# Attention's fixed order in a hybrid decoder layer: turning two steps ahead, scores five units ahead, gate sums apart, queries scaled later

## The chip, the cores and the metric

The kernel runs on one core of one Trainium2 chip. The metric is the device time of one launch in microseconds (us), the median of several runs. The core has a matrix engine (TensorE, PE in the rows; its weight loads are PEld), VectorE (DVE), ScalarE (ACT), GpSimd (POOL) and SyncE (SP), whose queue here issues the DMAs. TensorE writes its results into eight PSUM banks, from which VectorE and ScalarE copy them out.

## The reference

One decoder layer on 1024 tokens of width 1024, in float32:

```
xn   = RMSNorm(x)
proj = xn @ w_in      # attention q, k, v and gates | conv | memory q | 3 merge gates
A = attention over compressed blocks, selected blocks and a window of 512
B = causal depthwise convolution (31 taps), LayerNorm, swish, projection
C = cross-attention into 256 memory tokens
merged = sum over A, B, C of sigmoid(merge gate) * (branch @ its output weight)
h   = x + merged @ w_out
out = h + (silu(RMSNorm(h) @ w_gate) * (RMSNorm(h) @ w_up)) @ w_down
```

Attention has 8 query heads in 2 groups of width 64. With 1024 tokens all 16 selected blocks are taken, so the selected branch is causal attention over all keys. Each branch has its own softmax and its own gate.

## The kernel before, in words

Matrices are split into a high and a low float32r part, and each product is the sum of three products of parts (`mm3`, with `mm` in L153, the line that nearly every matmul has). A transpose is a matmul with the identity (`turn_in`, L733).

The stages are: projections and convolution taps, memory keys and values, memory attention, attention, merge of the three branches, output projection, and the feed-forward part (the last third of the span). The change is in the attention.

The attention works on 8 blocks of 128 tokens (i) times 2 head groups (g). Each (i, g) is a block of five **units**: branch 0 (compressed keys, all four heads at once), branch 1 (selected) in two head pairs, branch 2 (window) in two head pairs. A unit goes through these stations:

- **scores** (`scores`, L758): TensorE multiplies query tiles (`qt`) by keys, in chunks of up to 512 columns, into three PSUM banks (`at=0`). For branch 0 these are the compressed scores (`kcmp`, `qt`). VectorE adds the mask and takes the row minimum of the negated scores out of the bank (L810 and L780: the drains), ScalarE takes the exponential with a row sum (L815, L782), VectorE the reciprocal (L694), and GpSimd scales the tile (L699). The tiles lie in big buffers named `wsl` (three) and `slab`.
- **turning** (`turn_p`, L826): TensorE transposes the tile, two key blocks a **step**, into three other banks (`at=1`). ScalarE casts the high part (L132), VectorE subtracts to get the low part (L133), into a buffer `t`.
- **take** (`take`, L845): TensorE multiplies values by the turned step into the one output bank (`at=2`). The first take of a block is that of branch 0 (`vcmp`). After the last one of a block ScalarE copies half of the bank (L861), VectorE adds the rest (L864), and a DMA stores it to `od`.

Queries: `load_q` (L735) fetches the raw queries of a token block by DMA (L737) and scales them by their norms on VectorE (L738). `doubled` (L740) multiplies by the gain on GpSimd (L742), and `turn_q` (L746) transposes to `qt`. This happens within the window units of the block before.

**Fills.** The merge gates' projections (`gate_steps`, L705, 24 weight units of 128 columns, two halves each) have no hurry. The first 12 units are given to the scheduler with low priority (early gates). The other 12 (late gates) are 192 fill steps of three matmuls each. Eight steps, 24 matmuls, sum into the one bank `pf`; then ScalarE copies it out (L714, `fz`), and the next sum can begin. Their weights `fsl` are split by ScalarE and GpSimd (L133).

**The order.** Inside the attention TensorE's order is written out by hand (`in_row`, L146: each instruction is tied behind the one before). A plan lists entries. In an entry stand part of the scores of unit k, then the turning of the step after the one to be taken, then some fill steps, then one take step of unit k - LAG, with LAG = 4. Before unit 4 entries have no take. How many fill steps an entry gets follows from a level: each entry's own TensorE time is estimated, and fills raise the short ones to the same height (`share`). The other engines' orders are the scheduler's. Work of the next stage, the memory product (`wsl` by `slab`, L1011), is put between by the scheduler where the row's end comes near; its inputs go through the staging buffers `st`, which it shares with the query tiles.

Of the kernel before, what the change touches and what calls it, by code (L numbers as in the profile page):

```python
# [20 lines left out]
NT = S // P  # L21
KT = D // P
# [8 lines left out]
FILL, TAP = 2000000, 1000000  # L31
ORDER = mybir.DependencyInfo(mybir.DependencyClass.NoSync, mybir.DependencyReason.DATA)
N_EARLY = 12
LAG = 4
T_COL, T_MM, T_TURN = 1 / 2400, 0.0133, 0.112
TAP_LEAD = 12
N_MAIN, N_W, N_F = 16, 3, 2

# [2 lines left out]
def hybrid_layer_kernel(  # L41
# [48 lines left out]
    def t2(shape, dt=F32, p=P):  # L90
        return t2p.tile([p] + shape, dt, tag="t2", name=nm("t2"))

    def small(n):
        if n > 8:
            return smp.tile([P, n], F32, tag="smw", name=nm("smw"), bufs=3)
        return smp.tile([P, n], F32, tag="sm", name=nm("sm"))
# [3 lines left out]
    def bank(shape, dt=F32, p=P, at=None):  # L100
        if at is None:
            turn[1] += 1
            at = order[turn[1] % len(order)]
        return psp[at].tile([p] + shape, dt, tag=f"ps{at}", name=nm("ps"))
# [26 lines left out]
    def split(hi, lo, src, eng=None):  # L131
        m = nc.scalar.copy(hi, src)  # L132
        return m, (eng or nc.vector).tensor_tensor(lo, src, hi.bitcast(F32), op=OP.subtract)  # L133
# [18 lines left out]
    def mm(o, a, b, start, stop):  # L152
        m = nc.tensor.matmul(o, a, b, start=start, stop=stop)  # L153
        in_row(m)
        n = 1
        for d in o.shape[1:]:
            n *= d
        products.append((m.ins, n if a.dtype == F32R else 4 * n))
        return m
# [162 lines left out]
    def wide_proj(ws, t):  # L322

        o = bank([512])
        half, a = t // 4, (t % 4) * P
        if t == 0 and len(products) == 0:
            for k0 in (0, 4):
                for hx, hw in ((0, 0), (1, 0), (0, 1)):
                    for k in range(k0, k0 + 4):
                        mm(o, xn(hx, k, half, a, a + P), ws[k // 2][hw][:, k % 2, :], k + hx + hw == 0,  # L330
                           k == KT - 1 and hw == 1)
            return o
        for k in range(KT):
            hi, lo = ws[k // 2]
            mm3(o, xn(0, k, half, a, a + P), xn(1, k, half, a, a + P), hi[:, k % 2, :], lo[:, k % 2, :], k == 0, k == KT - 1)
        return o
# [50 lines left out]
    for u in range(2):  # L387
        w_ = slab([2, 2, 512])
        m, _ = split(w_[:, 0], w_[:, 1], raw_w[u])
# [268 lines left out]
    for t in range(NT):  # L658
        v = wide_proj(ws, t).rearrange("p (s a g d) -> p s a g d", s=2, a=2, g=2)
# [28 lines left out]
    def balanced(n):  # L688
        return [n] if n <= 4 else [n - n // 2, n // 2]
# [45 lines left out]
    def load_q(i):  # L735
        QN[i] = t2([8, 64])
        nc.sync.dma_start(QN[i].rearrange("p h d -> p (h d)"), qraw[1, i])  # L737
        nc.vector.tensor_tensor(QN[i], QN[i], rqn[:, i, :, None].to_broadcast([P, 8, 64]), op=OP.mult)  # L738

    def doubled(i, g):  # L740
        qd = t2([4, 2, 64])
        nc.gpsimd.tensor_tensor(qd, QN[i][:, 4 * g:4 * g + 4, None, :].to_broadcast([P, 4, 2, 64]),  # L742
                                gn[:, 0, None, None, :].to_broadcast([P, 4, 2, 64]), op=OP.mult)
        return qd

    def turn_q(i, g, qd):  # L746
        b = bank([4, P], at=1)
        for h in range(4):
            turn_in(b[:, h, :], qd[:, h].rearrange("p a d -> p (a d)"))
        QT = stage.tile([P, 2, 4, P], F32R, tag="st", name=nm("qt"))  # L750
        split(QT[:, 0], QT[:, 1], b)
        QS[(i, g)] = QT
# [5 lines left out]
    def scores(u, after):  # L758

        i, g, br, hp = u  # L760
        if br == 2:
            nxt = (i, 1) if g == 0 else (i + 1, 0)
            if hp == 0 and nxt[0] < NT:
                if g == 1 and nxt[0] + 1 < NT:
                    load_q(nxt[0] + 1)
                QD[nxt] = doubled(*nxt)
            if hp == 1 and nxt[0] < NT:
                turn_q(*nxt, QD.pop(nxt))
                yield
        QT = QS[(i, g)]  # L770
        if br == 0:
            mn_, den = small(4), small(4)
            b = bank([4, 64], at=0)
            for h in range(4):
                mm(b[:, h, :], QT[:, 0, h, :], kcmp[:, g * 64:(g + 1) * 64], True, False)
                mm(b[:, h, :], QT[:, 1, h, :], kcmp[:, g * 64:(g + 1) * 64], False, True)
            pc = t2([4, 64])
            tiles = [pc[:, h, :] for h in range(4)]
            for h in range(4):
                nc.vector.tensor_tensor_reduce(tiles[h], b[:, h, :], cmask[:, i, :], op0=OP.add, op1=OP.min,  # L780
                                               scale=-0.125, scalar=BIG, accum_out=mn_[:, h:h + 1])
                nc.scalar.activation(tiles[h], tiles[h], AF.Exp, scale=-1.0, bias=mn_[:, h:h + 1],  # L782
                                     accum_out=den[:, h:h + 1])
            softmax_tail(i, g, br, 0, den, tiles)
            after.append((u, tiles))
            yield
            return
        K = KSW[br - 1]
        k0 = 0 if br == 1 else max(0, i - 4)
        nb = i + 1 - k0  # L790
        turn[0] += 1
        pt = (wslab if turn[0] % 5 < 3 else slab)([2, S], F32)
        tiles = [pt[:, h, :nb * P] for h in range(2)]
        mn_, den = small(4), small(2)
        ch = balanced(nb)
        for h in range(2):
            kb, last = k0, None
            for ci, n in enumerate(ch):
                b = bank([512], at=0)[:, :n * P]
                mm(b, QT[:, 0, 2 * hp + h, :], K[:, g, kb * P:(kb + n) * P], True, False)  # L800
                mm(b, QT[:, 1, 2 * hp + h, :], K[:, g, kb * P:(kb + n) * P], False, True)
                if ci == len(ch) - 1:
                    m = strip[:, 768 - n * P:]
                elif br == 2:
                    m = strip[:, :n * P]
                else:
                    m = strip[:, P:(n + 1) * P]
                acc = mn_[:, 2 * h + ci:2 * h + ci + 1]
                o = (kb - k0) * P
                nc.vector.tensor_tensor_reduce(tiles[h][:, o:o + n * P], b, m, op0=OP.add, op1=OP.min,  # L810
                                               scale=-0.125, scalar=BIG if last is None else last, accum_out=acc)
                last = acc
                kb += n
                if ci == len(ch) - 1:
                    nc.scalar.activation(tiles[h], tiles[h], AF.Exp, scale=-1.0, bias=last, accum_out=den[:, h:h + 1])  # L815
                    if h == 1:
                        softmax_tail(i, g, br, 2 * hp, den, tiles)
                        after.append((u, tiles))
                yield

    def turns_of(u):

        nb = nblocks(u)
        return [0] if u[2] == 0 else [min(2, nb - j) for j in range(0, nb, 2)]
# [57 lines left out]
    plan, steps = [], [(u, s) for u in units for s in range(len(turns_of(u)))]  # L882

    def step_time(u, s):
        n = turns_of(u)[s]
        return 4 * T_TURN + 4 * P * T_COL + T_MM if n == 0 else 2 * n * T_TURN + 2 * n * (2 * P * T_COL + T_MM)

    for k in range(len(units) + LAG):
        at = atoms_of(units[k]) if k < len(units) else []
        mine = list(range(len(turns_of(units[k - LAG])))) if k >= LAG else []  # L890
        m = max(1, len(mine)) if mine else len(at)
        for j in range(m):
            part = at[j * len(at) // m:(j + 1) * len(at) // m]
            v = (units[k - LAG], mine[j]) if mine else None
            plan.append((k, len(part), v, sum(part) + (step_time(*v) if v else 0.0)))

    late = (3 * KT - N_EARLY) * 2 * KT
    room = 3 * late * (4 * P * T_COL + T_MM)
# [8 lines left out]
    for _, _, _, c in plan:  # L907
        run += max(0.0, hi_ - c)
        share.append(min(late, int(late * run / room + 0.5)))

    load_q(0)
    load_q(1)
    QD[(0, 0)] = doubled(0, 0)
    row[0] = keys_done
    turn_q(0, 0, QD.pop((0, 0)))
    fills, filled = late_gates(), 0
# [8 lines left out]
    at_step = 0  # L925
    for (k, n_at, v, _), upto in zip(plan, share):
        for _ in range(n_at):
            next(streams[k])
        if v is not None:
            for n in ((0, 1) if at_step == 0 else (at_step + 1,)):  # L930
                if n < len(steps):
                    turn_step(n)
        for _ in range(filled, upto):
            next(fills)
        filled = upto
        if v is not None:
            take(*v, turned.pop(at_step))
            at_step += 1
# [459 lines left out]
```

## Time and profile before

| | |
|---|---|
| median of 3 runs | 1743.81 us (1742.79 to 1748.59) |
| profiled execution | 1743.21 us, span 1741.5 us |
| granted TensorE clock | 1.00 |
| bytes moved by DMA | 211.83 MB |
| attention's row | about 490 to 885 us of the span |

The profile's page gives each engine's busy time. The views of windows, waits, timeline and chain answer for a stretch: busy time by engine, who ended whose idle time, the instructions in order, and the chain of work that ended last. In a row, `out<-in` are the tiles by name, `x6` is the number of merged instructions, and a bracket gives the idle time before the first of them and what ended it. The busy time of a run of matmuls includes the tail of its last one.

### The profile page before, as it was taken

The page shows a single profiled execution, that of the slowest core. Times are in us where ns is not written, and L with a number is a line of the kernel's source. Part 1 is how long each engine was busy: PE and PEld are TensorE (multiplying, and loading weights), DVE is VectorE, ACT ScalarE, POOL GpSimd, SP SyncE. Part 2 cuts the span into 40 slices and gives each one's busy share as a digit, 9 for nine tenths or more (in the row PEclk, how much of TensorE's full clock was granted, in tenths as well). Part 3 has the DMA queues.
Part 4 walks back from the last instruction along what each step waited for, and adds up shares of the span by engine and source line. Part 5 has one row for each costly group of instructions (what it writes and reads, how often), then busy time and mean ns, then how long its engine had stood idle before and what let it go on. Part 6 is the DMA issues. An engine that isn't in the chain of part 4 may idle for free.

```text
span 1741.5 us, 23348 instructions
## 1 busy us (share of the span) xinstructions
PE 1694.7 (97%) x8520; PEld 1420.8 (82%) x8520; DVE 1077.9 (62%) x1839; ACT 736.5 (42%) x1376; POOL 515.1 (30%) x478
## 2 busy tenths in 40 slices
PE   7999999999988999999999999999999999999999
PEld 6887898888767888888888878878888888888887
DVE  6288887687227676766666535765545555457655
ACT  7311534342237766666555424532322322234332
POOL 0000002120136444434103510366556677410000
PEclk9999999999999999999999999999999999999999
DMA  8012433321221111011565413233332445794773
GB/s 275 33 39 85 164 117 119 104 92 47 67 76 41 43 38 55 28 37 50 169 209 169 156 57 107 97 109 109 97 127 91 158 147 174 250 394 149 230 232 123
DMA packets 176729, 211.83 MB, mean 122 GB/s; under 512 B 11284, under 2 KB 113988, under 8 KB 175590
## 3 DMA queue, kind: packets, MB, share of 16 engines
q1 hardware_dynamic: 176614, 210.34, 36.5%
q8 instruction: 67, 1.10, 0.3%
q14 instruction: 48, 0.39, 0.1%
HBM read 155.77 MB, written 54.53 MB: 121 GB/s over the span
## 4 chain that ended last, share of the span: by engine, by line
PE 56%; DVE 5%; ACT 4%; issue 3%; DMA 3%; POOL 1%; ACTq 0%; DVEq 0%; SPq 0%; POOLq 0%
PE ps L153 31%; PE ps L1332 11%; PE pf L153 10%; PE ps L733 3%; PE pf L1332 1%; DMA t<-zd 1%; POOL slab L1020 1%; ACT slab L132 1%; DVE wsl L810 1%; DVE slab L133 1%; DVE t L864 1%; DMA st<-in_w_nsa_out_dram 1%; ACT slab L815 0%; ACT t L132 0%; DMA st<-md 0%
## 5 line engine op out<-in xcount | busy, mean ns | idle before, releaser
L153 PE MATMUL ps<-slab,wsl 128*128 128x512 f32 (+1 forms) x1652 | 368.3, 381 | 1.6 <-DMA wsl<-in_cmp_w_dram 0.9
L153 PEld LDWEIGHTS ps<-slab,wsl 128*128 128x128 f32 x1652 | 300.0, 188 | 63.0 <-issue 1.7
L153 PE MATMUL pf<-slab,fsl 128*128 128x512 f32 x1236 | 334.9, 404 | 13.7 <-ACT fz L714 13.7
L153 PEld LDWEIGHTS pf<-slab,fsl 128*128 128x128 f32 x1236 | 218.3, 189 | 56.0 <-ACT fz L714 20.1
L1228 DVE TENSOR_TENSOR t<-ps,t 128x512 f32<-128x512 f32 x130 | 88.7, 687 | 108.0 <-PE ps L153 104.6
L428 DVE SCALAR_TENSOR_TENSOR slab<-slab,cw 128x1023 f32<-128x1023 f32 (+14 forms) x120 | 152.1, 1267 | 2.1
L133 DVE TENSOR_TENSOR t<-ps,t 128x512 fp32r<-128x512 f32 (+2 forms) x192 | 120.2, 632 | 52.5 <-ACT t L132 49.8
L153 PE MATMUL ps<-slab,fsl 128*128 128x512 f32 x636 | 149.0, 391 | 1.6 <-DVE slab L133 1.6
L132 ACT CAST t<-ps 128x512 fp32r<-128x512 f32 (+2 forms) x192 | 101.9, 537 | 106.4 <-PE ps L733 86.6
L153 PE MATMUL ps<-wsl,slab 128*128 128x512 f32 (+1 forms) x648 | 140.3, 361 | 1.8 <-ACT slab L132 1.7
L153 PEld LDWEIGHTS ps<-slab,fsl 128*128 128x128 f32 x636 | 119.2, 188 | 27.6 <-DVE slab L133 2.0
L153 PEld LDWEIGHTS ps<-wsl,slab 128*128 128x128 f32 x648 | 108.0, 189 | 19.4 <-ACT slab L132 2.1
L153 PE MATMUL ps<-t,slab 128*128 128x256 f32 (+1 forms) x672 | 120.0, 294 | 1.7 <-DVE t L133 1.1
L153 PEld LDWEIGHTS ps<-t,slab 128*128 128x128 f32 x672 | 104.7, 188 | 19.8 <-DVE t L133 5.5
L1332 PE MATMUL ps<-wsl 128*128 128x512 f32 x495 | 118.7, 389 | 0.0
L153 PE MATMUL ps<-slab,slab 128*128 128x512 f32 x480 | 115.8, 392 | 1.7 <-ACT slab L231 1.3
L600 POOL TENSOR_SCALAR t<-t,sm 128x256 f32<-128x256 f32 x32 | 25.5, 815 | 291.2 <-DVE sm L596 261.6
L1332 PEld LDWEIGHTS ps<-wsl 128*128 128x128 f32 x495 | 92.9, 188 | 19.3
L153 PEld LDWEIGHTS ps<-slab,slab 128*128 128x128 f32 x480 | 89.3, 188 | 21.5 <-ACT slab L231 2.2
L133 DVE TENSOR_TENSOR wsl<-st,wsl 128x1024 fp32r<-128x1024 f32 x58 | 74.5, 1284 | 32.3 <-ACT wsl L132 32.1
L153 PE MATMUL ps<-slab,qt 128*128 128x384 f32 (+3 forms) x384 | 87.6, 333 | 6.5 <-DVE sm L810 6.2
L132 ACT CAST wsl<-st 128x1024 fp32r<-128x1024 f32 x59 | 61.8, 1050 | 72.1 <-PE ps L153 41.5
(245 smaller groups left out, 2719.8 us busy)
## 6 DMA issues: line engine op xcount, KB each, us to landing
t<-in_w_down_dram SPq DMA_DIRECT2D x70, 256.0 KB, 3.6
fst<-in_w_in_dram SPq DMA_DIRECT2D x24, 512.0 KB, 3.7
zd<-fz SPq DMA_DIRECT2D x48, 256.0 KB, 2.0
t<-zd SPq DMA_DIRECT2D x24, 512.0 KB, 3.9
st<-in_w_gate_dram SPq DMA_DIRECT2D x22, 512.0 KB, 3.7
st<-in_w_up_dram SPq DMA_DIRECT2D x22, 512.0 KB, 4.2
ad<-t SPq DMA_DIRECT2D x44, 256.0 KB, 2.6
st<-in_w_in_dram SPq DMA_DIRECT2D x20, 512.0 KB, 3.8
```

The source lines that it names most:

```text
L132: m = nc.scalar.copy(hi, src)
L133: return m, (eng or nc.vector).tensor_tensor(lo, src, hi.bitcast(F32), op=OP.subtract)
L153: m = nc.tensor.matmul(o, a, b, start=start, stop=stop)
L428: return nc.vector.scalar_tensor_tensor(acc[:, s:], u[:, :S - s], cw[:, ct, 30 - s:31 - s], acc[:, s:], op0=OP.mult, op1=OP.add)
L600: nc.gpsimd.tensor_scalar(pm[:, tt, h, :], pm[:, tt, h, :], rec[:, j:j + 1], 1.0, op0=OP.mult, op1=OP.mult)
L733: in_row(nc.tensor.transpose(o, i, ident))
L810: nc.vector.tensor_tensor_reduce(tiles[h][:, o:o + n * P], b, m, op0=OP.add, op1=OP.min, scale=-0.125, scalar=BIG if last is None else las ...
L864: nc.vector.tensor_tensor(oT[par * 64:(par + 1) * 64], o[0:64].rearrange("p (a b) q -> p a b q", b=2)[:, :, par, :], bot[:, :, par, :], op ...
L1020: nc.gpsimd.tensor_tensor(a, a, z, op=OP.add)
L1228: nc.vector.tensor_tensor(o, a_, b_, op=OP.add)
L1332: nc.tensor.matmul(B[t], a_, b_, start=start and k == 0 and j == 0, stop=k == FH - 1 and j == 2, skip_group_check=True)
```

## The change

- `LAG` goes from 4 to 5: scores of unit k stand beside the takes of unit k - 5, which is the same unit of the block before.
- `LEAD = 2`: the step turned in an entry is the second one after the step taken, not the next one.
- `LEAVE = 0.9`: in the plan the entry with a block's first take (but for the very first block) counts 0.9 us less, so it gets more fill steps.
- A run of fill steps stops where a gate's sum is complete (`filled % KT`); steps left over go to the next entry. A run may still begin at such a place.
- The scaling of raw queries leaves `load_q` for `scale_q`, which is called half a block later, in the first window unit of group 0; the DMA stays where it was.

```diff
-LAG = 4
-T_COL, T_MM, T_TURN = 1 / 2400, 0.0133, 0.112
+LAG, LEAD = 5, 2
+T_COL, T_MM, T_TURN, LEAVE = 1 / 2400, 0.0133, 0.112, 0.9
...
         nc.sync.dma_start(QN[i].rearrange("p h d -> p (h d)"), qraw[1, i])
+
+    def scale_q(i):
         nc.vector.tensor_tensor(QN[i], QN[i], rqn[:, i, :, None].to_broadcast([P, 8, 64]), op=OP.mult)
...
                 if g == 1 and nxt[0] + 1 < NT:
                     load_q(nxt[0] + 1)
+                if g == 0 and 0 < i < NT - 1:
+                    scale_q(i + 1)
                 QD[nxt] = doubled(*nxt)
...
-            plan.append((k, len(part), v, sum(part) + (step_time(*v) if v else 0.0)))
+            first_of_block = v is not None and v[0][2] == 0 and v[0][:2] != (0, 0)
+            plan.append((k, len(part), v, sum(part) + (step_time(*v) if v else 0.0) - (LEAVE if first_of_block else 0.0)))
...
         if v is not None:
-            for n in ((0, 1) if at_step == 0 else (at_step + 1,)):
+            for n in (range(LEAD + 1) if at_step == 0 else (at_step + LEAD,)):
                 if n < len(steps):
                     turn_step(n)
-        for _ in range(filled, upto):
+        here = filled
+        while filled < upto and (filled == here or filled % KT):
             next(fills)
-        filled = upto
+            filled += 1
```

Three places of TensorE's order show what moves. The first is the end of block (4, 0), where the next block's queries are turned and the new block's output bank begins. In the rows, `ps` with `qt` are scores, `ident` transposes, `pf` gate sums, `vcmp` a first take, and `ps` with `t` and `slab` other takes. Before:

```order
L733 MATMUL ps_5810<-ident,t_975_5637 64x128 x4
L153 MATMUL pf_5615<-slab_194,fsl_5130 128x512 x3
L153 MATMUL ps_5600<-t_1010_5787,slab_2629 128x256 x4
L733 MATMUL ps_5831<-ident,t_1003_5768 128x128 x4
L153 MATMUL ps_5842<-slab_2627,qt_5572 128x384 x2
L153 MATMUL ps_5846<-slab_2627,qt_5572 128x256 x2
L153 MATMUL ps_5851<-slab_2627,qt_5572 128x384 x2
L153 MATMUL ps_5855<-slab_2627,qt_5572 128x256 x2
L733 MATMUL ps_5864<-ident,slab_5664 128x128 x4
L153 MATMUL ps_5872<-t_1015_5815,vcmp 128x512
L733 MATMUL ps_5874<-ident,slab_5664 128x128 x4
L153 MATMUL pf_5615<-slab_195,fsl_5130 128x512 x3
```

And now:

```order
L733 MATMUL ps_5831<-ident,t_1003_5777 128x128 x4
L153 MATMUL ps_5842<-slab_2627,qt_5573 128x384 x2
L733 MATMUL ps_5846<-ident,t_972_5637 64x128 x4
L153 MATMUL ps_5666<-t_1010_5796,slab_2629 128x256 x4
L153 MATMUL ps_5858<-slab_2627,qt_5573 128x256 x2
L153 MATMUL ps_5863<-slab_2627,qt_5573 128x384 x2
L153 MATMUL ps_5867<-slab_2627,qt_5573 128x256 x2
L733 MATMUL ps_5876<-ident,slab_5668 128x128 x4
L153 MATMUL ps_5666<-t_1015_5821,slab_2629 128x256 x4
L153 MATMUL ps_5896<-kcmp,qt_5836 128x64 x8
L733 MATMUL ps_5920<-ident,slab_5668 128x128 x4
L153 MATMUL pf_5688<-slab_401,fsl_5006 128x512 x6
```

The four score chunks no longer stand in one piece: a transpose and a take come behind the first. The compressed scores (`kcmp`) of the next block now stand before its first take, which follows the last row here, with six gate matmuls ahead of it.

The second place is the change from one gate sum to the next, early in the row. Before:

```order
L153 MATMUL pf_4112<-slab_194,fsl_3995 128x512 x3
L153 MATMUL pf_4112<-slab_195,fsl_3995 128x512 x3
L153 MATMUL ps_4161<-t_623_4218,slab_2629 128x256 x2
L153 MATMUL ps_4268<-slab_2627,qt_4124 128x128 x2
L153 MATMUL ps_4273<-slab_2627,qt_4124 128x128 x2
L733 MATMUL ps_4282<-ident,t_612_4174 64x128 x4
L153 MATMUL pf_4112<-slab_195,fsl_3995 128x512 x3
L153 MATMUL pf_4296<-slab_399,fsl_3995 128x512 x3
```

And now:

```order
L153 MATMUL pf_4120<-slab_195,fsl_3995 128x512 x6
L153 MATMUL ps_4167<-kcmp,qt_4112 128x64 x8
L733 MATMUL ps_4192<-ident,t_564_3972 64x128 x4
L733 MATMUL ps_4200<-ident,wsl_4002 128x128 x2
L733 MATMUL ps_4206<-ident,wsl_4037 128x128 x2
L153 MATMUL ps_4212<-t_611_4197,vcmp 128x512
L153 MATMUL ps_4217<-slab_2626,qt_4112 128x128 x2
L153 MATMUL ps_4222<-slab_2626,qt_4112 128x128 x2
L733 MATMUL ps_4231<-ident,slab_4075 128x128 x2
L153 MATMUL pf_4237<-slab_399,fsl_3995 128x512 x6
```

Before, `pf_4296` follows `pf_4112` at once. Now eight rows stand between the two sums. In the same piece is the attention's opening: three steps are turned one after the other, and the first take (`vcmp`) follows with no fill between.

The third place is where the memory product (`ps` with `slab_8549` and `wsl_8569`) enters the row. Before:

```order
L733 MATMUL ps_8393<-ident,wsl_8128 128x128 x4
L153 MATMUL pf_8385<-slab_192,fsl_8074 128x512 x3
L153 MATMUL ps_8303<-t_1572_8376,slab_2628 128x256 x4
L733 MATMUL ps_8408<-ident,wsl_8128 128x128 x4
L153 MATMUL pf_8385<-slab_193,fsl_8074 128x512 x6
L153 MATMUL ps_8616<-slab_8549,wsl_8569 128x512 x3
```

And now:

```order
L153 MATMUL ps_8317<-t_1568_8342,slab_2628 128x256 x4
L733 MATMUL ps_8385<-ident,wsl_8067 128x128 x4
L153 MATMUL ps_8616<-slab_8549,wsl_8569 128x512 x2
L153 MATMUL pf_8393<-slab_192,fsl_8107 128x512 x6
L153 MATMUL ps_8317<-t_1570_8357,slab_2628 128x256 x4
L733 MATMUL ps_8404<-ident,wsl_8067 128x128 x4
```

The product's first matmuls stand two gate steps and a take earlier, and in smaller pieces.

More of the change, by code (lines that the diff above doesn't have):

```diff
@@ L909, in hybrid_layer_kernel @@
         share.append(min(late, int(late * run / room + 0.5)))
-    load_q(0)
-    load_q(1)
+    for i in range(2):
+        load_q(i)
+        scale_q(i)
     QD[(0, 0)] = doubled(0, 0)
```

## The prediction

> **What bounds the kernel now.** I read the page first, then the stages, then who waits for whom, then TensorE's rows in order of time.
>
> ```profile
> span 1741.5 us, 23348 instructions
> PE 1694.7 (97%) x8520; PEld 1420.8 (82%) x8520; DVE 1077.9 (62%) x1839; ACT 736.5 (42%) x1376; POOL 515.1 (30%) x478
> ```
>
> TensorE is busy 97% of the span and no other engine above 62%, so a change that adds no matmuls can only gain TensorE's idle time. The change touches the attention alone, so I ask how much of that lies there. The next view gives each engine's busy time by stretch (TensorE first, granted clock third from the end).
>
> ```profile
> 490.00:580.00 90.00, 80.14 (x497) 68.35 (x497) 54.01 (x217) 58.97 (x188) 46.15 (x75) 1.00 0.18 55
> 580.00:842.00 262.00, 251.50 (x1606) 220.57 (x1606) 181.53 (x565) 172.68 (x400) 115.59 (x136) 1.00 0.14 42
> 842.00:885.00 43.00, 41.61 (x230) 35.19 (x231) 24.07 (x36) 21.51 (x32) 2.85 (x4) 1.00 0.61 199
> 885.00:1013.00 128.00, 126.94 (x553) 103.32 (x551) 87.55 (x104) 68.98 (x74) 46.00 (x32) 1.00 0.52 172
> ```
>
> The attention's row runs from 490 to 885 us. TensorE is idle 9.86 + 10.50 + 1.39 = 21.75 us in it, but only 1.06 us in the 128 us behind it, where it stays the bound: what the row gains is kept. Who ended the idle time in 490 to 885 (sum, times, longest):
>
> ```profile
> PE pf L153 <- ACT fz L714: 8.8, 11, 1.6
> PE ps L153 <- DVE sm L810: 6.2, 6, 2.1
> PE ps L153 <- DVE t L864: 3.8, 5, 1.5
> PE ps L153 <- DVE t L133: 2.0, 4, 0.9
> PE ps L153 <- DVE qt L133: 1.2, 2, 0.9
> ```
>
> 28 waits, 22.0 us: all of it has a name, and each name answers to an edit. The method is one for all: a wait's **need** is its **cover** (the TensorE work that stands between the two ends of the dependency) plus the idle time measured. From the new order I take the new cover; what the need exceeds it by, remains. Covers use these spacings, start to start (TensorE's rows: start, busy time, line, operation, idle time before it and who ended that; the last row is from the chain):
>
> ```profile
> 455.98 5.72 PE L153 MATMUL pf<-slab,fsl 128*128 128x512 f32 x24
> 462.42 5.73 PE L153 MATMUL pf<-slab,fsl 128*128 128x512 f32 x24 [0.72 <-ACT fz L714]
> 631.84 0.64 PE L153 MATMUL ps<-t,slab 128*128 128x256 f32 x4
> 632.31 0.60 PE L733 MATMUL ps<-ident,t 128*128 128x128 f32 x4
> 632.66 1.19 PE L153 MATMUL ps<-slab,qt 128*128 128x384 f32 x6
> 635.01 0.50 PE L153 MATMUL ps<-slab,qt 128*128 128x256 f32 x2 [1.16 <-DVE sm L810]
> 1147.57 19.04 PE ps L153 x84
> ```
>
> Three gate matmuls 0.71 (24 in 5.72), four takes 0.47, four transposes 0.35, a pair of scores about 0.3. The chain's row shows 84 undisturbed matmuls in 19.04, so 24 need 5.44; the 24 from 455.98 are followed 6.44 later. A wait of 0.72 thus costs 1.00: every wait costs some 0.28 beyond its idle time.
>
> **1. Merge-gate sums never back to back.** The gates have one PSUM bank; at a change of sums ScalarE must copy it out first.
>
> ```profile
> 497.18 1.65 PE L153 MATMUL pf<-slab,fsl 128*128 128x512 f32 x6 [0.72 <-ACT fz L714]
> 518.07 0.97 PE L153 MATMUL pf<-slab,fsl 128*128 128x512 f32 x3 [1.00 <-ACT fz L714]
> 578.14 0.96 PE L153 MATMUL pf<-slab,fsl 128*128 128x512 f32 x3 [0.16 <-ACT fz L714]
> 758.22 0.96 PE L153 MATMUL pf<-slab,fsl 128*128 128x512 f32 x3 [0.47 <-ACT fz L714]
> 854.13 0.96 PE L153 MATMUL pf<-slab,fsl 128*128 128x512 f32 x3 [0.82 <-ACT fz L714]
> ```
>
> Of the 8.8 us, 1.62 stands at 490.03, where the last early gate meets the first late one; no edit reaches it. Six changes have nothing between them (the first, third and last of these rows are three; the other three 0.72, 0.67 and 1.34): 5.27 us. Of the 17 changes with other work between, four still wait (the first and last are shown; 0.16, 0.58, 0.71, 0.47): 1.92, or 0.11 each. So 0.9 us of other work does not always cover it. The new order has two changes with only a score pair (0.13) or four transposes (0.35) between, in the opening without takes: they keep 0.59 + 0.37. The other 21 have 0.59 us or more, at 0.11 each 2.4. So 7.19 becomes 3.3: **3.9 gained**, between 0 (all 21 wait like the four) and 6.2.
>
> **2. Scores five units ahead.** Scores use three banks. At 632.66, three chunks go out and the fourth, 635.01, waits for VectorE to empty the first: query transposes and four chunks stood in one entry of the plan. Their cover was two score pairs, 0.59. Eight such places, five waited (1.16, 0.84, 0.84, 0.77, 0.44): 4.05. With unit k beside unit k-5, scores meet as many takes as before but evenly; the smallest cover at these places is 1.41. Needs 1.75, 1.43, 1.43, 1.36, 1.03 leave 0.4: **3.65 gained**.
>
> The sixth is another matter (VectorE's, GpSimd's and TensorE's rows, then all scalings with shortest, median and longest in ns):
>
> ```profile
> 537.11 2.15 DVE L738 TENSOR_TENSOR t<-t,rqn 128x512 f32<-128x512 f32 x1 [0.44 <-DMA t<-qraw]
> 536.33 2.37 POOL L133 TENSOR_TENSOR fsl<-fst,fsl 128x1024 fp32r<-128x1024 f32 x1
> 539.72 0.50 PE L153 MATMUL ps<-slab,qt 128*128 128x256 f32 x2 [2.15 <-DVE sm L810]
> L738 DVE TENSOR_TENSOR t<-t,rqn x8: 679/682/2145, 446.2 to 700.2; 128x512 f32<-128x512 f32 x8
> ```
>
> The query scaling took 2.15 instead of 0.68 while GpSimd ran a weight split until 538.70; the scores behind it came late. The DMA held VectorE only 0.44. **Raw queries a block ahead** therefore removes at most that 0.44. The fetch keeps its place in SyncE's queue; only VectorE's scaling moves, by half a block, and GpSimd's doubling, which needs it, comes five units later, so nothing waits there. Whether it meets a split again I can't read from the order: between 0 and 2.15, I take 1.1. The Trainium skill (SBUF — State Buffer, "SBUF: two separate sides") says that a VectorE operation with two SBUF inputs and a GpSimd operation that reads SBUF take one shared port pair as an exclusive lock. The trace agrees at 537.11; by that rule fetching earlier frees nothing, and this term would be 0.
>
> **3. The extra gate work ahead of a block's first take** (LEAVE). That take needs the one output bank, which VectorE empties after the block before.
>
> ```profile
> 532.61 0.47 PE L153 MATMUL ps<-t,vcmp 128*128 128x512 f32 x1 [0.61 <-DVE t L864]
> 545.80 0.47 PE L153 MATMUL ps<-t,vcmp 128*128 128x512 f32 x1 [0.52 <-DVE t L864]
> 558.08 0.48 PE L153 MATMUL ps<-t,vcmp 128*128 128x512 f32 x1 [0.86 <-DVE t L864]
> 615.65 0.47 PE L153 MATMUL ps<-t,vcmp 128*128 128x512 f32 x1 [1.47 <-DVE t L864]
> 843.15 0.48 PE L153 MATMUL ps<-t,vcmp 128*128 128x512 f32 x1 [0.39 <-DVE t L864]
> ```
>
> Covers go 1.89 to 2.59, 1.89 to 2.59, 1.41 to 1.70, 1.65 to 1.87, 1.53 to 2.49. Left are 0.57 and 1.25 of 3.85: **2.0 gained** (bounds 0.5 if VectorE comes later by one 0.69 split, 3.8).
>
> **4. Turning two steps ahead.** A take waits for the cast and subtraction of its transposed tile.
>
> ```profile
> 509.09 0.50 PE L153 MATMUL ps<-t,vcmp 128*128 128x512 f32 x1 [0.91 <-DVE t L133]
> 560.33 0.63 PE L153 MATMUL ps<-t,slab 128*128 128x256 f32 x3 [0.74 <-DVE t L133]
> 521.97 0.97 PE L153 MATMUL ps<-kcmp,qt 128*128 128x64 f32 x7 [0.34 <-DVE qt L133]
> 547.19 0.97 PE L153 MATMUL ps<-kcmp,qt 128*128 128x64 f32 x7 [0.88 <-DVE qt L133]
> ```
>
> The usual cover rises from about 2.0 to 4.0, so three of the four waits go. The first grows: the opening turns three steps and takes at once, cover 0.89 before, 0.35 now, so 0.91 becomes 1.45. Net **0.55 gained**. The compressed scores of the next block wait for its query tiles (the last two rows; covers 1.40 and 1.83, needs 1.74 and 2.71). Here the covers fall: 1.41, 1.85, 1.41 and 1.62 in the third to sixth block, 3.0 to 5.5 later (7 to 8 before in the last). At a need near 2.0 that is 1.7 instead of 1.2: **0.5 lost** (bounds 0.4 and 3.4, with 2.0 and 2.5 as needs).
>
> What I cost at nothing: buffers. One more scored tile is alive, on three big buffers; between the last transpose that frees one and the first score that refills it TensorE has 2.7 us of work at least (4.5 before), so VectorE doesn't meet a full pool. Of four buffers for turned tiles three are held instead of two, and the fourth is free one take earlier than it is needed. If either cover were gone, VectorE would stand for a transpose's 0.35 us, with the score drains behind it.
>
> **5. Waits that go take their 0.28 along.** Some 12 of the 28 go: at 0.25, **3.0 gained**.
>
> **6. The first memory product.** It stands inside the row.
>
> ```profile
> 842.16 0.60 PE L733 MATMUL ps<-ident,wsl 128*128 128x128 f32 x4
> 854.44 1.05 ACT L132 CAST wsl<-st 128x1024 fp32r<-128x1024 f32 x1 [0.36 <-DMA st<-in_w_mem_out_dram]
> 858.85 1.54 PE L153 MATMUL ps<-slab,wsl 128*128 128x512 f32 x6
> ```
>
> The last score ends at 842.16; that frees staging buffers for loads, and the weight's cast ends at 855.49, 13.3 later. Cover was 13.7 of work; the new order puts the product 11.2 of work behind the last score. With about 1 us of waits left in between, **1.1 lost** (0 if the first load's split, which now stands ahead of the last scores, starts the chain earlier; 5.5 if it takes the whole 16.7 to 858.85).
>
> Sum: 3.9 + 3.65 + 1.1 + 2.0 + 0.55 - 0.5 + 3.0 - 1.1 = 12.6 us. The profiled execution took 1743.21 us (1.71 outside its span), 0.60 below the median of 1743.81. 1743.21 - 12.6 = 1730.6; beside the median 1731.2. I predict **1731**.
>
> **The rivals.**
> *Early blocks stay as they are.* In 490 to 580 ScalarE is busy 58.97 of 90 us, and in its worst stretch
>
> ```profile
> 540.00:560.00 20.00, 17.32 (x118) 15.05 (x117) 16.30 (x60) 17.20 (x52) 11.97 (x22) 1.00 0.16 43
> ```
>
> 86%, VectorE 82%. If they set the pace there, the 9.86 us stay. Behind 580 remain 3.0 (bank changes), 3.65, 0.6 and 2.0 for eight waits' tails, less 1.1: 8.2, giving 1735.6. Against it: the waits there end singly, with TensorE busy between.
> *Nothing is gained.* Every wait moves behind the next dependency, as the four spaced bank changes hint: 1743.8.
> *All named waits go* but 1.62: 20.4, and 27 tails of 0.25, less 1.1: 26, giving 1718. Speaks against it: needs above 2.6 in two of five output-bank waits.
> *Slower: the queries' wait.* Casts and subtractions of two steps now stand ahead of the query tile's on ScalarE and VectorE. If its need rises to N in all blocks, the covers of part 4 (1.41, 1.85, 1.41, 1.62, then 2.99, 3.20, 3.44, 3.03, then 4.85 or more) cost at N = 5 us 13.7 + 7.3 + 0.6 = 21.6, against 13.1 gained otherwise: 1752. It is slower by more than 0.3% from N = 4.7. The largest need seen is 2.71, and one more subtraction is 0.69, so this is unlikely.
>
> **How the numbers follow.** Forecast (1725 to 1736) 0.62; early blocks unchanged (1734 to 1741) 0.15; nothing 0.10; all waits gone (below 1725) 0.08; slower 0.05. The range takes in the second and most of the fourth: 1720 to 1742. About 0.3%, 5.2 us, is what a measurement of this kernel can tell from no change. Faster by more: 0.62 + 0.08 + 0.13 = 0.83; same 0.02 + 0.10 = 0.12; slower 0.05.
>
> **What would show it.** In the profile after: TensorE's idle time between the first scores and the row's end near 12 us instead of 21.75; waits for the gate copy about 5 (the 1.6 at the early gates' end among them), no score wait over 0.5 in blocks from the fifth on, output-bank waits about 1.8, one take wait of 1.4 at the start, query waits in blocks three to six. A wait of 1 us at the first memory product. Total TensorE matmuls unchanged. I am wrong if the covers grew and the idle time stayed, or if it moved behind 885 us.

## The result: 22 us faster, and the profile after

| | before | after |
|---|---|---|
| median | 1743.33 us (1742.79 to 1748.59, 4 runs) | 1720.67 us (1720.28 to 1722.43, 4 runs) |
| ratio | 1 | 0.9865, 95% interval 0.9845 to 0.9886 |
| span of the profiled execution | 1741.5 us | 1718.8 us |

The direction was right, the size was not: 22.7 us went where 12.6 were forecast. The measured 1720.67 us lies below the range of 1725 to 1736, where the prediction had put a chance of 0.08. The page of after, its span and its engines' busy times:

```profile
span 1718.8 us, 23356 instructions
PE 1689.1 (98%) x8520; PEld 1423.7 (83%) x8520; DVE 1078.7 (63%) x1839; ACT 737.1 (43%) x1376; POOL 517.9 (30%) x478
```

The matmuls are the same 8520 and the other engines do the same work. The 22.7 us are 46.8 - 29.7 = 17.1 less idle time of TensorE, and 5.6 less **busy** time for the same matmuls. To see where, two stretches are compared that begin at the same gate sum and end at the same product of the output projection (the first `fsl` by `slab`). First the stretch of before, then that of after, with the columns of the prediction's second view:

```profile
490.03:1007.02 516.99, 495.26 (x2860) 423.68 (x2861) 343.04 (x914) 320.82 (x690) 206.06 (x241) 1.00 0.28 89
```

```profile
489.81:986.28 496.47, 488.26 (x2860) 424.64 (x2861) 345.90 (x918) 322.26 (x692) 211.65 (x244) 1.00 0.29 93
```

Both hold 2860 matmuls. 516.99 - 496.47 = 20.5 us were gained here: TensorE's idle time went from 21.7 to 8.2 us (13.5), and 7.0 us went out of its busy time. The rest lies outside: 0.2 ahead of it, 2.0 behind it. The waits that are left in after, as the prediction listed those of before (who waits for whom: sum, times, longest; the added lines shift the numbers, so L810, L815, L864 and L1020 of before are L814, L819, L868 and L1027 here):

```profile
PE pf L153 <- ACT fz L714: 3.9, 7, 1.6
PE ps L153 <- DVE qt L133: 2.2, 3, 1.1
PE ps L153 <- DVE t L133: 1.4, 1, 1.4
PE ps L153 <- DVE t L868: 1.3, 2, 0.8
PE ps L153 <- ACT wsl L132: 0.4, 1, 0.4
PE ps L153 <- DVE sm L814: 0.2, 1, 0.2
```

The signs named in the prediction are nearly all there: one take wait of 1.4 us at the start, query waits in the third, fifth and sixth block, no score wait over 0.5. Most sums are a little smaller than forecast (the query waits are larger, 2.2 us for 1.7), and these 9.4 us (22.0 before) explain only 12.6 us of the gain. The other part shows in the same view for the weight loads (PEld). Before:

```profile
PEld pf L153 <- ACT fz L714: 13.0, 12, 2.0
PEld ps L153 <- DVE sm L810: 10.1, 12, 2.3
PEld ps L153 <- DVE t L133: 6.9, 13, 1.4
PEld ps L153 <- DVE qt L133: 2.0, 3, 1.1
```

After:

```profile
PEld pf L153 <- ACT fz L714: 6.1, 8, 2.0
PEld ps L153 <- DVE qt L133: 2.8, 4, 1.2
PEld ps L153 <- DVE t L133: 1.7, 1, 1.7
PEld ps L153 <- DVE sm L814: 1.4, 3, 0.6
```

With the smaller rows, 38.6 us in 48 waits became 17.0 us in 25. The matmuls of before had four waits for turned tiles (2.0 us); their weight loads had 13 (6.9 us). What the nine others look like, in before, first TensorE's matmuls and then its weight loads at the same moment:

```profile
666.79 1.00 PE L153 MATMUL ps<-t,slab 128*128 128x256 f32 x4
667.63 0.27 PE L733 MATMUL ps<-ident,wsl 128*128 128x128 f32 x1
```

```profile
666.57 0.19 PEld L153 LDWEIGHTS ps<-t,slab 128*128 128x128 f32 x1
667.17 0.42 PEld L153 LDWEIGHTS ps<-t,slab 128*128 128x128 f32 x3 [0.41 <-DVE t L133]
```

The first take uses the high part of the turned tile and runs; the second waits 0.41 us for the low part. From 666.79 to 667.63 four takes need 0.84 us, not the 0.47 of an undisturbed place. No matmul row says that TensorE was idle: the time counts as busy. Three score entries did the same, for example (matmuls, then weight loads, of before):

```profile
662.55 1.75 PE L153 MATMUL ps<-slab,qt 128*128 128x384 f32 x8
664.14 0.38 PE L733 MATMUL ps<-ident,wsl 128*128 128x128 f32 x2
```

```profile
663.80 0.30 PEld L153 LDWEIGHTS ps<-slab,qt 128*128 128x128 f32 x2 [0.39 <-DVE sm L810]
```

And of after, half of such an entry without a wait:

```profile
819.96 0.75 PE L153 MATMUL ps<-slab,qt 128*128 128x384 f32 x4
820.55 0.60 PE L733 MATMUL ps<-ident,wsl 128*128 128x128 f32 x4
```

Four score matmuls take 0.59 us there, so eight would take 1.18; those at 662.55 took 1.59.

The 2.0 us behind the row are one wait in the output projection. TensorE's row at its end, then ScalarE's last merge cast ahead of it, in before:

```profile
1013.60 0.74 PE L153 MATMUL ps<-wsl,slab 128*128 128x512 f32 x2 [1.66 <-ACT slab L132]
```

```profile
1012.93 0.62 ACT L132 CAST slab<-slab 128x512 fp32r<-128x512 f32 x1 [2.25 <-POOL slab L1020]
```

And that cast in after:

```profile
987.69 0.62 ACT L132 CAST slab<-slab 128x512 fp32r<-128x512 f32 x1 [2.28 <-POOL slab L1027]
```

The merge came 25.2 us earlier. The chain of work that ended in this wait shows why. It leaves TensorE at the end of the attention's row, with the last gate sum, and goes over ScalarE's copy of that sum and over the copy and the store of the attention's last output (`od`). From there it runs over the merge's loads, casts and additions alone. Two of its rows in before (start, time, what):

```profile
883.68 0.58 ACT fz L714
885.78 4.18 DMA od<-t
```

In after the same copy stands at 858.4, 25.3 us earlier. The projection came only 20.7 us earlier, since more of the memory product now stands behind the attention's last take and covers the merge. TensorE's first rows behind that take, in before:

```profile
883.71 5.64 PE L153 MATMUL ps<-slab,wsl 128*128 128x512 f32 x24
```

And in after:

```profile
857.31 11.30 PE L153 MATMUL ps<-slab,wsl 128*128 128x512 f32 x49
```

### The profile page after: what moved, and what is told of

It reads as the page before. It is cut to its first block, busy times and chain, and to the rows that moved or that the text cites. A ratio compares the mean times of both kernels' runs of the same rounds, so it can differ in the third digit from the quotient of the medians.

```text
span 1718.8 us, 23356 instructions
## 1 busy us (share of the span) xinstructions
PE 1689.1 (98%) x8520; PEld 1423.7 (83%) x8520; DVE 1078.7 (63%) x1839; ACT 737.1 (43%) x1376; POOL 517.9 (30%) x478
## 4 chain that ended last, share of the span: by engine, by line
PE 67%; DVE 2%; ACT 2%; issue 1%; DMA 0%; POOL 0%; ACTq 0%; DVEq 0%; POOLq 0%
PE ps L153 39%; PE pf L153 12%; PE ps L1339 11%; PE ps L733 4%; PE pf L1339 1%; DVE slab L133 1%; ACT slab L819 0%; ACT fz L714 0%; ACT t L132 0%; DMA st<-in_w_mem_out_dram 0%; DVE wsl L814 0%; PE ps L240 0%; ACT slab L132 0%; DVE t L868 0%; ACT wsl L819 0%
## 5 line engine op out<-in xcount | busy, mean ns | idle before, releaser
L153 PEld LDWEIGHTS pf<-slab,fsl 128*128 128x128 f32 x1236 | 219.0, 189 | 49.9 <-ACT fz L714 13.2
L153 PEld LDWEIGHTS ps<-t,slab 128*128 128x128 f32 x672 | 103.8, 189 | 13.5
L153 PEld LDWEIGHTS ps<-slab,slab 128*128 128x128 f32 x480 | 91.0, 191 | 21.3 <-ACT slab L231 1.8
L132 ACT CAST wsl<-t 128x1024 fp32r<-128x1024 f32 x42 | 44.2, 1053 | 100.7 <-POOL t L129 38.9
```

## The experiments

Two theories stood against each other. **A**: the edits lean on one another, and a wait is worth what the whole order's covers leave, with stalls that no matmul row records. **B**: each edit is worth the waits that carry its name in the trace of before. Five kernels undo one edit in after, three make one edit alone in before, three go beyond after. The ratios are to before on the same chip. Differences to after are between medians, and the ratios give the same within 0.2 us; differences to before are those of the ratio.

**No stop at a gate sum's end** (`u_bank`, against after):

```diff
-        here = filled
-        while filled < upto and (filled == here or filled % KT):
+        for _ in range(filled, upto):
             next(fills)
-            filled += 1
+        filled = upto
```

> The changed kernel with one edit undone: gate work is again dealt out without a stop at the end of a merge-gate sum. Theory A (the edits lean on one another; what counts is the cover that the whole order leaves): in this order only 3 sums in the attention stand back to back, not 6, because the other edits already pull them apart; each costs about 0.9 us idle and 0.35 beyond it, and two short covers go, so +2.3 us: 1723. Theory B (each edit is worth the waits that carry its name in the trace of before): gate-copy waits return from 3.9 to 8.8 us with their ends, +7 us: 1727.5.

0.9887 (0.9874 to 0.9901), 1723.2 us: 2.8 above after's median of 1720.4 (measured again, below); the intervals overlap. Its gate-copy waits:

```profile
PE pf L153 <- ACT fz L714: 5.7, 8, 1.6
```

A's place: 5.7 us, not B's 8.8. In this order the other edits pull most sums apart already. Not all of the 2.8 us are gate waits: these rose by 1.8 us (from 3.9), the wait at the first memory product by 1.3 (from 0.4), and the output bank's fell by 0.5.

**Scores four units ahead** (`u_lag`):

```diff
-LAG, LEAD = 5, 2
+LAG, LEAD = 4, 2
```

> The changed kernel with scores four units ahead again. Both theories: eight places with a cover of 0.59 us between a score bank's drain and its next use return, about 4 us of idle time and 0.37 beyond it at each of the eight (also where no idle time is recorded), +7.0. Theory A: the query tiles' covers grow from 1.3-3.1 to 2-8 us, so their 2.2 us of waits go with their ends (-3), and the opening take's 1.4 wait goes (-1.7): +2.5 in sum, 1723. Theory B: nothing else moves, and the 2.15 us wait behind the slow query scaling returns too: +9.4, 1730.

0.9919 (0.9906 to 0.9933), 1728.7 us, 8.3 more than after. B came nearer in size, but not by its mechanism: no score wait is longer than 0.8 us, so the long one behind the query scaling did not return. The rows that did:

```profile
PE ps L153 <- DVE sm L814: 3.6, 7, 0.8
PE ps L733 <- POOL wsl L699: 1.6, 3, 1.1
PE ps L733 <- DVE qt L133: 1.5, 1, 1.5
```

The score banks wait as both theories said. What A had left out is new: transposes (L733) wait for GpSimd's scaling of the tile (L699) and behind a query split. Turned two ahead, a tile scored only four units ahead is not ready. The two numbers are one choice.

**Turning one step ahead** (`u_lead`):

```diff
-LAG, LEAD = 5, 2
+LAG, LEAD = 5, 1
```

> The changed kernel with the turning one step ahead. Theory A: with five units of lead and one of turning, the compressed scores come 0.5-0.95 us of work behind the query transposes in most blocks, and the need seen is 1.7 to 2.65 us, so 12 to 14 query waits of about 1.2 us with 0.25 beyond: +15 us or more, about 1736; the waits for turned tiles stay below 1 us in all. Theory B: only the waits for turned tiles return (0.6 us, and 3 ends of 0.25), less the query waits that the lead of two brought: +0 to 1.4, 1721.

0.9917 (0.9904 to 0.9931), 1728.3 us, 7.9 more than after. Neither theory's numbers fit. A's query waits did not come (1.9 us, two times): the covers named there had been counted from the transposes of the compressed probabilities, not from the queries'. The takes wait instead:

```profile
PE ps L153 <- DVE t L133: 5.6, 6, 1.6
PE ps L153 <- DVE qt L133: 1.9, 2, 1.1
```

So this edit holds back 4.2 us of take waits (1.4 in after) where before had 2.0 in all; the gate-copy waits are 2.0 us longer too.

**No credit** (`u_leave`):

```diff
-T_COL, T_MM, T_TURN, LEAVE = 1 / 2400, 0.0133, 0.112, 0.9
+T_COL, T_MM, T_TURN, LEAVE = 1 / 2400, 0.0133, 0.112, 0.0
```

> The changed kernel without the credit that puts extra gate work ahead of a block's first take. Theory A: the output bank's cover is 1.16 us or less at eight of 15 places (1.4 at the least before), against needs of 1.9 to 3.1 seen: about 1 us and 0.25 beyond at each, +8 us: 1729. Theory B: the output-bank waits return from 1.3 to 3.85 us, three more of them with ends of 0.3: +3.5, 1724.

0.9948 (0.9936 to 0.9961), 1733.7 us, 13.3 more than after: A's mechanism, more than its size.

```profile
PE ps L153 <- DVE t L868: 9.8, 12, 1.4
```

Twelve output-bank waits, where before had five and after has two. This is the dearest edit of all, and its price is not in the trace of before.

**After once more** (`after2`):

> The changed kernel once more, as the mark for the others on this chip: 0.9865 of before by both theories.

0.9872 (0.9858 to 0.9885), 1720.4 us.

**Five units alone** (`a_lag`, against before):

```diff
-LAG = 4
+LAG = 5
```

> The kernel before with one edit alone: scores five units ahead. Theory A (the edits lean on one another): the score banks' waits go (6.2 us idle, 2.0 at their ends, 1.3 of unrecorded stalls: -9.4), but the output bank's cover falls to 1.16 us at nine of 15 places, which in the kernel without the credit made 12 waits of 9.8 us and 3.4 at their ends instead of 5.1 in all (+8), and the takes' cover shrinks as in the kernel with the turning one step ahead (5.6 + 1.6 instead of 3.0: +4): no gain, 1744 beside 1742. Theory B (each edit is worth its own waits of before): -9.4, 1732.5.

0.9991 (0.9982 to 1.0): A. The score banks' 6.2 us are gone, and the output bank took them:

```profile
PE pf L153 <- ACT fz L714: 9.6, 12, 1.6
PE ps L153 <- DVE t L864: 9.2, 14, 1.5
PE ps L153 <- DVE sm L810: 0.2, 1, 0.2
```

A's third term, 4 us more at the takes, did not come: their waits are 1.5 us (2.0 before).

**Two steps alone** (`a_lead`, against before):

```diff
-            for n in ((0, 1) if at_step == 0 else (at_step + 1,)):
+            for n in ((0, 1, 2) if at_step == 0 else (at_step + 2,)):
```

> The kernel before with one edit alone: the turning two steps ahead. Theory A: also the stalls go that only the weight loads' waits show (takes that are 0.3 to 0.4 us longer than undisturbed ones, ten places, 3.3 us), with three of four recorded waits (1.1 us) and their ends (0.8): -5.2, 1737. Theory B: only the recorded waits go: -1.1 to -1.9, 1740.5.

0.9981 (0.9972 to 0.9989), 3.3 us less than before: between the two. The weight loads' waits for turned tiles fell from 6.9 to 0.5, as A had it, but others grew:

```profile
PEld ps L153 <- DVE t L133: 0.5, 1, 0.5
PEld ps L733 <- POOL t L699: 3.2, 10, 0.7
```

GpSimd's scaling again, ten times.

**The credit alone** (`a_leave`, against before):

```diff
+            first_of_block = v is not None and v[0][2] == 0 and v[0][:2] != (0, 0)
-            plan.append((k, len(part), v, sum(part) + (step_time(*v) if v else 0.0)))
+            plan.append((k, len(part), v, sum(part) + (step_time(*v) if v else 0.0) - (0.9 if first_of_block else 0.0)))
```

> The kernel before with one edit alone: the credit ahead of a block's first take. Theory A: all output-bank waits go, with their ends and three unrecorded stalls (3.85 + 1.26 + 1.0: -6), since covers rise to 1.9 to 3.0 everywhere: 1736. Theory B: recorded waits go down to 1.8 as forecast, with two ends: -2.6, 1739.5.

0.9942 (0.9929 to 0.9954), 10.1 us less: more than both. All the waits of TensorE that are left in it from 488 to 1005 us:

```profile
PE pf L153 <- ACT fz L714: 7.8, 8, 1.6
PE ps L153 <- DVE t L133: 3.7, 10, 1.0
PE ps L153 <- DVE sm L810: 3.1, 6, 0.8
PE ps L153 <- ACT slab L132: 1.0, 1, 1.0
```

Output-bank waits: none. Query waits: none either, which neither theory had. Four units behind the scores, a block's first take stands in the entry that begins with the next block's query transposes; the credit puts one or two more gate steps (0.7 us each) between these and the compressed scores that need them. With five units the first take's entry holds the compressed scores themselves, ahead of the gate work, and this use of the credit is lost. The score waits halved, mostly because the 2.15 us one is gone.

**Queries scaled at once** (`u_scale`, against after):

```diff
                 if g == 1 and nxt[0] + 1 < NT:
                     load_q(nxt[0] + 1)
-                if g == 0 and 0 < i < NT - 1:
-                    scale_q(i + 1)
+                    scale_q(nxt[0] + 1)
```

> The changed kernel with one edit undone: VectorE scales a block's raw queries right behind their fetch again. TensorE's and GpSimd's order stay the same. Theory A: the 2.15 us scaling of before was a meeting of that moment, since the wait behind it is gone in the kernels that have only the five units or only the credit; nothing returns, or up to 0.7 us where VectorE stands for the fetch: 1720.5 to 1721. Theory B: the stretched scaling and the score wait behind it return with their end: +2.4, 1723.

0.9871 (0.9856 to 0.9886): A. This edit gave nothing that can be measured.

**An opening turned earlier** (`x_turn`, against after): steps 0 and 1 are turned in the entries of units 3 and 4.

```diff
+        if v is None and k >= LAG - LEAD and k - LAG + LEAD not in turned:
+            turn_step(k - LAG + LEAD)
         if v is not None:
-            for n in (range(LEAD + 1) if at_step == 0 else (at_step + LEAD,)):
+            for n in (at_step + LEAD,):
```

> The changed kernel with the opening's first two turned tiles made ahead of the first take's entry. Theory A: the opening take's wait goes (1.42 us and 0.25 behind it) and nothing else moves: 0.9990 of the changed kernel, 1718.8. Theory B: the opening is bound by ScalarE and VectorE, and the wait moves to the query tiles or a gate copy behind it: no change, 1720.5.

0.9859 (0.9843 to 0.9876), 1719.0 us. The 1.4 us wait is gone and no other grew by more than 0.1 us, as A said; the difference to after is within the intervals.

**Queries a unit earlier as well** (`x_both`, with `x_turn`'s edit; the plan's estimate for the query transposes, in `atoms_of`, moves along):

```diff
-        if br == 2:
-            nxt = (i, 1) if g == 0 else (i + 1, 0)
-            if hp == 0 and nxt[0] < NT:
+        nxt = (i, 1) if g == 0 else (i + 1, 0)
+        if br == 1 and hp == 1:
+            if nxt[0] < NT:
...
-            if hp == 1 and nxt[0] < NT:
-                turn_q(*nxt, QD.pop(nxt))
-                yield
+        if br == 2 and hp == 0 and nxt[0] < NT:
+            turn_q(*nxt, QD.pop(nxt))
+            yield
```

> As the one before, and the query tiles doubled, transposed and split one unit earlier. Theory A: the three query waits go too (2.2 us and 0.66 behind them), since their cover rises from 1.3 to 2.7 at a need of 1.7 to 2.65: about 1716. Theory B: the transposes then stand ahead of VectorE's score drains of another unit and a score or output-bank wait takes their place: 1718.5 to 1720.

0.9864 (0.9849 to 0.9879), 1719.6 us: B. The query waits are gone; gate, output and score banks took their place:

```profile
PE pf L153 <- ACT fz L714: 4.9, 7, 1.6
PE ps L153 <- DVE t L868: 1.7, 3, 0.8
PE ps L153 <- DVE sm L814: 1.3, 2, 0.7
```

**A credit of 1.2 on top** (`x_l12`): in `x_both`, `LEAVE` is 1.2.

> As the one before, with a credit of 1.2 instead of 0.9. Theory A: four of the output bank's short covers rise by 0.7, so its two waits (1.3 and 0.5 behind) and about half of four unrecorded stalls of 0.3 go: 1714 to 1715. Theory B: gate work is scarce in the last blocks and other covers pay for it: 1716 to 1718.

0.9837 (0.9822 to 0.9851), 1714.5 us: A's time, and the fastest kernel here, 6 us under after. All that is left from 488.9 us to the row's end:

```profile
PE pf L153 <- ACT fz L714: 3.7, 5, 1.6
PE ps L153 <- DVE t L868: 1.3, 4, 0.4
PE ps L153 <- DVE sm L814: 0.5, 1, 0.5
```

The mechanism is only in part A's. The output bank's waits, which A let go, fell from 1.7 to 1.3 us; those for the gate copies fell by 1.2 us and for the score banks by 0.8. Whether 1.2 would do the same without the earlier queries is open: no run has it.

All kernels together: what each saved in the whole launch (one less its ratio, times 1742.6 us), and how much less than in before TensorE's matmuls and its weight loads waited from 488 us to the row's end, in us. Here after is the run `after2` for the saving and the first trace of after for the waits.

| kernel | saved | matmuls' waits | weight loads' waits |
|---|---|---|---|
| after | 22.3 | 12.6 | 21.6 |
| u_bank | 19.7 | 10.1 | 18.8 |
| u_lag | 14.1 | 7.7 | 13.6 |
| u_lead | 14.5 | 7.2 | 16.7 |
| u_leave | 9.1 | 3.9 | 11.5 |
| a_lag | 1.6 | -1.0 | 3.8 |
| a_lead | 3.3 | 0.7 | 2.6 |
| a_leave | 10.1 | 7.4 | 10.8 |
| u_scale | 22.5 | 12.1 | 21.3 |
| x_turn | 24.6 | 13.9 | 23.4 |
| x_both | 23.7 | 13.2 | 22.8 |
| x_l12 | 28.4 | 16.5 | 28.1 |

The weight loads' waits give the saving within 2.4 us in every kernel. The savings' own intervals are 1.5 to 2.9 us to either side, and for `a_lag` and `a_lead` 2.4 us is as much as the saving. The matmuls' waits fall short of it by 2.6 to 11.9. The traces of `a_lag`, `a_lead` and `u_leave` show a granted clock of 0.99 from 490 to 850 us, all others 1.00, so a small part of their waits can be the clock's.

## Why the forecast was too small, step by step

It was too small at three places: the recorded waits (12.6 us went, 9.6 forecast), what goes beyond them in the row (20.5 - 12.6 = 7.9, forecast 3.0 as **step 5**), and the wait behind the row (2.0, forecast 0, with 0.2 ahead of the row). That is 3.0 + 4.9 + 2.2 = 10.1 us.

**Step 5 failed most**, with the premise that it rests on. "28 waits, 22.0 us: all of it has a name" took the recorded idle time for all of TensorE's loss, and the step priced only the ends of these waits, 12 of them at 0.25. That part was nearly right: 13 went, and an end is worth about 0.3 on the mean. What it put at nothing are stalls without a recorded wait. Set against the undisturbed spacing of each kind of matmul, the trace of before has 20 of them over 0.2 us, 6.6 us in all, and after has seven, 2.0 us: that is 4.6 of the 7.9 us. The weight loads' waits had shown this before the change: 38.6 us, not 22.0. The method of covers and needs served, but it was fed with the matmul rows alone.

**Step 1, gate sums** (3.9 forecast): 7.19 became 2.3, so 4.9. Only six changes wait besides the first, none over 0.55; the two in the opening kept 0.55 and 0.28 (forecast 0.59 and 0.37). The size was right within 1.0, but `u_bank` shows that the stop at a sum's end owns only some 1.8 us of it; the plan's other numbers part most sums. Of the five rows that this step shows, the second (1.00), not the third (0.16), is a change with nothing between; the sums 5.27 and 1.92 are right.

**Step 2, score banks** (3.65 and 1.1): 6.2 became 0.2. The entries with query transposes and four chunks gave what was forecast (4.05 became 0.2), and the three of the eight places that had no recorded wait had each lost 0.4. The long wait at the slow scaling went whole. It didn't go by the raw queries' edit, though: `u_scale` gives the same time without it, and `a_leave`, where the scaling stands where it stood, has none of it. The moment shifted, and in after, `u_scale` and `a_leave` no scaling meets a weight split. The prediction had also drawn a value of 0 for this edit from the Trainium skill's rule on the shared port ("SBUF: two separate sides" in SBUF — State Buffer). That value came out, but `u_scale` does not test the rule, since no scaling meets a split there either.

**Step 3, the credit** (2.0): the output bank gave 2.55, near the forecast in sum, but by luck in its places. The fifth block's first take kept nothing (0.57 forecast) and the eighth's 0.45 (1.25 forecast). The seventh's waits 0.85 us in after; it had no recorded wait in before, so the step gave it no need. As the worth of the credit this was far off: 10.1 us alone, 13.3 when undone. Compared between before and after, the bank's waits hide that five units alone raise them from 3.8 to 9.2 us, which the credit then removes. The sum of the forecast was not hurt by this, since it was made against the whole order; any statement on which edit pays would have been.

**Step 4, turning and queries** (0.55 gained, 0.5 lost): recorded 0.6 gained, 1.0 lost. The query waits' bounds (0.4 and 3.4) do not follow from their needs: by the covers shown, 2.0 gives a loss of 0.5 and 2.5 one of 2.5. The opening's wait of 1.42 against 1.45 forecast is the best hit: need and cover, nothing else. The lead's real gain was among the unrecorded stalls: weight loads' waits for turned tiles 6.9 to 1.7.

**Step 6, the memory product** (1.1 lost): 0.4 recorded, at 833.4 us.

**Behind the row** the forecast said that "what the row gains is kept". It was kept and more: a stretch with 1.06 us of idle time was given no chance to improve. That 1.06 us is the start of this very wait, which the stretch's end at 1013 cut off: TensorE's last matmul ends at 1011.94 and the next begins at 1013.60. The merge's chain, which ended 1.7 us too late, hangs on the end of the attention's row and not on what TensorE does behind it.

**The rivals.** The named waits went except 9.4 us, so "all named waits go" (1718) was nearest in time and wrong in mechanism: it let go 20 us of recorded idle time, and 12.6 went. "Early blocks stay as they are" fell: from 490 to 580 us TensorE's busy time was 80.14 us before, and in after

```profile
490.00:580.00 90.00, 84.46 (x524) 74.23 (x524) 53.98 (x227) 61.92 (x198) 50.72 (x78) 1.00 0.19 61
```

with ScalarE busier than before, so it had not set the pace. The longest query wait was 1.12 us, in the sixth block with its cover of 1.62: a need of 2.74, beside 2.71 before. The slower rival's 4.7 never came near.

Of the edits, summed alone the three give 15.0 us, undone one by one the four (with the gate sums' stop, which no run has alone) are worth 32.3; together they gave 22.3. Neither sum is the gain: five units save 1.6 us alone but cost 8.3 when undone, two steps 3.3 and 7.9.

## What to carry to other kernels

Before pricing a change on a saturated TensorE, read the waits of its weight loads beside those of its matmuls: here they told the gain within 2.4 us in twelve kernels, and the matmuls' idle time told about half of it in most. Where an order is written by hand, look at the smallest cover of every dependency in the whole new order, not at the waits of the old one: a lead that is lengthened alone moves its wait to the next bank. And test edits both alone and undone, since either by itself misjudges them.

## What the runs showed of the hardware

TensorE's busy time is no fixed cost: the same 2860 matmuls were busy 495.3 us before and 488.3 us after at a granted clock of 1.00, while their weight loads were busy 423.7 and 424.6. The Trainium skill warns of this (Perfetto Trace Analysis, "Identifying the Most-Contended Engine"): matmul busy time is a poor measure of how close a kernel is to its peak, because matmuls are pipelined, and the weight loads' busy share is one of two that it names as better. The trace agrees: in a stretch that became 4.0% shorter, the share of weight loads rose from 82.0% to 85.5%, when the matmuls' share went from 95.8% to 98.3%.

The query scaling stretched against GpSimd's small scalings too (VectorE's row, then GpSimd's, of after):

```profile
637.18 1.28 DVE L740 TENSOR_TENSOR t<-t,rqn 128x512 f32<-128x512 f32 x1
```

```profile
636.18 1.75 POOL L699 TENSOR_SCALAR wsl<-wsl,sm,gsb 128x640 f32<-128x640 f32 x2
```

It took 1.28 us instead of 0.68, and TensorE didn't wait for it. GpSimd's two took their usual 0.88 us each. In `a_lag` the same operations met with the other outcome: VectorE's scaling, from 645.37, took 0.72 us, and the second of GpSimd's two, from 645.29, took 1.39 us. So here one of the two engines kept its time and the other was held up, and not always the same one.
